# Three FFN heads put in order by hand: side 3's sums ahead of the tail, weight loads by free room, GpSimd's accumulating loads ahead of its power

## The chip, the cores and the metric

The kernel runs on one core of a Trainium2 chip. The metric is the device time of one execution in microseconds (us), the median of several executions. A core has five engines with a queue of instructions each, which go in order within an engine and wait for each other by semaphores: TensorE (PE; its weight loads are shown as PEld), VectorE (DVE), ScalarE (ACT), GpSimd (POOL) and SyncE (SP). Here SyncE issues the plain DMA loads, and GpSimd issues those that add to what lies in the buffer already (accumulating loads).

## The reference

A trunk of four layers on a sequence of 512 tokens with 1024 channels. Each layer is a mixer (S5 state space, gated linear attention (GLA), differential attention, S5 again) and an FFN, all float32:

```python
for layer in range(4):
    h = rmsnorm(x, norm_mix[layer]);  x = x + mixer(h)
    h = rmsnorm(x, norm_ffn[layer])
    g, u = split(h @ w_gate_up, 2)          # 1024 x (2 x 2816)
    x = x + (silu(g) * u) @ w_down          # 2816 x 1024
return rmsnorm(x, norm_final)
```

## The kernel before

Every float32 matrix is split into a rounded half and the residue (`halves`: a ScalarE cast and a VectorE subtraction, into a `whl` buffer, five of them), and a product is three TensorE matmuls: high by high, high by low, low by high.

The gate and up products of the FFN of layers 1, 2 and 3 are done by a scheme with seven products where plain blocking has eight. The activations, transposed, lie in four quarters `F[(0,0)]`, `F[(0,1)]`, `F[(1,0)]`, `F[(1,1)]` of a tile that the trace calls `halves`; `a11`, `a12`, `s` and `a22` are names for them. Seven combinations of the quarters, the sides "11", "12", "1", "2", "3", "4", "22", are split once per layer (`parts`, called by `side`). `total(name)` makes the sums by VectorE in place: "1" is `s - a22`, "2" then `s - a11`, "4" then `s + a12`. Before, "3" is made after "1" and "2", as `-s - a22`, in two buffers `s3`.

The weights go by 11 blocks of 256 hidden channels. A block has five weight tiles of 512 KB, loaded by `load(name, q, half, plus, room)`: "11", "21" and "22" are plain quarters; "1" and "3" are a plain load by SyncE (the base) and then an accumulating load by GpSimd that adds another quarter. "11" and "3" go into `wst` (three buffers), the others into buffers from the list `slots`, or into a given `room`. `added` adds "22" to "1" and `four` adds "21", on GpSimd for blocks 0 and 1 and on VectorE for the rest. `one`, `two`, `five`, `six`, `seven`, `three`, `four` are the seven products; `one_out`, `five_out`, `six_out` copy their sums out of PSUM. `one`, `six`, `seven` and `four` of a block use the PSUM bank `a`, `five` and `three` bank `c`, `two` bank `d`; in the trace all are on line 505.

The head of an FFN is the stretch from the last evacuations of the mixer's output projection (its tail; `add_x` calls `take` for each 128x512 piece of `x`) to the middle of block 2. In it the order is written out by hand (`self.hand(...)` opens the guard, an empty `self.hand()` ends it), for TensorE, ScalarE, VectorE and SyncE. GpSimd's order there, and all orders after it, are a scheduler's. The layer's row scale (`finish`: the mean square, then a power on GpSimd, line 124), its diagonal (`diag`) and its spread over the rows (`spread`, `rows`) lie between the products of blocks 0 and 1. `left.ahead(n)` loads and splits "11" of blocks 0 and 1 while the projection runs; the class is `Sides`, a `Left` with `early = True`.

At the start of `ffn` block 0's and block 1's tiles are loaded: block 0's "21" and "1" into slots, its "22" into the first half of a tile `lent`; block 1's "21" into the last slot, "1" into the second half of `lent`, "22" into the tile of the norm's gain, which is free after the last `take`. When the head is over, `halves` and the gain tile join the slots (`freed`), and block 2's "1" goes into `F[(0,1)]`, which `total("4")` is the last to read. In layer 2, `turn_x` stores `x` to DRAM and loads it back in another order by GpSimd's queue (`xturn`, 2 MB each way).

Of the kernel before, what the change touches and what calls it, by code (L numbers as in the profile page):

```python
# [11 lines left out]
F32 = mybir.dt.float32  # L12
# [4 lines left out]
ALU = mybir.AluOpType  # L17
# [4 lines left out]
P = 128  # L22
D = 1024
SEQ = 512
NT = SEQ // P
# [35 lines left out]
class Left:  # L61
# [15 lines left out]
    def room(self):  # L77
        self.hT = [self.tr.hp.tile([P, KT, SEQ], F32R, tag="hT", name=f"hT{z}") for z in range(2)]
# [14 lines left out]

    def square(self, t, d):
        tr = self.tr
        junk = tr.np_.tile([P, 512], F32, tag="h", name="sq")
        tr.nc.scalar.activation(
            junk[:], tr.x[:, t, d * 512 : (d + 1) * 512], AF.Square, scale=1.0 / 32.0,
            accum_out=self.ms[:, d, t : t + 1],
        )  # L100
# [25 lines left out]
    def diag(self):  # L126
        tr = self.tr
        nc = tr.nc
        self.dg = diag = tr.np_.tile([P, NT, P], F32, tag="h", name="diag")
        for t in range(NT):  # L130
            nc.vector.tensor_scalar(diag[:, t], tr.ident[:], self.r[:, t : t + 1], None, op0=ALU.mult)

# [11 lines left out]
class Sides(Left):  # L144
# [18 lines left out]
    def ahead(self, n):  # L163

        E = mybir.EngineType
        if not self.heads:
            self.tr.hand(E.PE, E.Activation, E.DVE, E.SP)
        w = [self.tr.staged(self.quarter(0, 0, b), 4, 256) for b in range(len(self.heads), len(self.heads) + n)]
        self.heads += [self.tr.halves(y, 4, 256) for y in w]

    def open(self, pool, names):

        for n in names:
            self.place[n] = pool.tile([P, 2, 4, 256], F32R, name="side" + n)
# [15 lines left out]
    def total(self, name):  # L190

        v = self.tr.nc.vector
        a11, a12, s, a22 = (self.F[k] for k in ((0, 0), (0, 1), (1, 0), (1, 1)))
        if name == "3":
            self.us = []
            for k in (0, 2):
                u = self.tr.np_.tile([P, 2, 256], F32, tag="h", name="s3")
                v.scalar_tensor_tensor(u[:], s[:, k : k + 2], -1.0, a22[:, k : k + 2], op0=ALU.mult, op1=ALU.subtract)
                self.us.append(u)
        else:  # L200
            y, op = {"1": (a22, ALU.subtract), "2": (a11, ALU.subtract), "4": (a12, ALU.add)}[name]
            v.tensor_tensor(s, s, y, op=op)
# [10 lines left out]
class Trunk:  # L213
# [81 lines left out]
    def gemm_b(self, stat, w, nk, c0, evac, k0=0, tail=0, between=(), ahead=None):  # L295
# [22 lines left out]
        if tail:  # L318
            hls = [self.wb(w, k0 + kb, c0) for kb in range(nk - tail, nk, 2)]
            if ahead:  # L320
                ahead()
            for t in range(NT):
                for j in range(tail):
                    k = nk - tail + j
                    self.mm3(
                        accs[t][:], stat(k, 0, t), stat(k, 1, t), hls[j // 2][:, 0, j % 2],
                        hls[j // 2][:, 1, j % 2], k == 0, k == nk - 1,
                    )
                evac(t, accs[t])
# [180 lines left out]
    def seven_block(self, fp, slots, left, wgu, b, turn):  # L510
# [3 lines left out]
        v = nc.vector  # L514
        A = left.place
        T = lambda name: fp.tile([P, 512], F32, tag="r1" if name == "r1" else "glu", name=name, bufs=2 if name == "r1" else 3)
        W, H, bank, keep, lent = {}, {}, {}, {}, set()
# [6 lines left out]
        def load(name, q, half, plus=None, room=None):  # L524
            if name in ("11", "3"):
                W[name] = self.staged(left.quarter(q, half, b), 4, 256)
            else:
                W[name] = slots.pop(0) if room is None else room
                if room is not None:
                    lent.add(name)  # L530
                nc.sync.dma_start(W[name][:], left.quarter(q, half, b))
            w = W[name]
            if plus:
                self.added = nc.gpsimd.dma_start(w[:], left.quarter(*plus, b), accum_op=ALU.add)
# [11 lines left out]
        def direct():  # L546
            load("11", 0, 0)

        def roomed(sums=None, rest=None):

            load("21", 1, 0)
            load("1", 0, 1, (0, 0), sums)
            load("22", 1, 1, None, rest)

        def summed():
            load("3", 0, 1, (1, 1))
# [50 lines left out]
        def four():  # L607
# [18 lines left out]
            return act  # L626

        return dict(
            split=split, direct=direct, roomed=roomed, summed=summed, one=one, one_out=one_out, two=two,
            two_out=two_out, gate1=gate1, five=five, five_out=five_out, added=added, six=six, six_out=six_out,  # L630
            seven=seven, three=three, four=four,
        )

    def ffn(self, l, left, after=None, turn=False, aside=None):

        i = self.i
        wgu, wd = i["ffn_w_gate_up"][l], i["ffn_w_down"][l]
        nxt = None
        r = left.r
        with self.tc.tile_pool(name=f"ffn{l}", bufs=1, reuse_waits="tile") as fp:  # L640

            room = lambda: fp.tile([P, 2, 4, 256], F32, tag="act", name="lent", bufs=4)
            left.open(fp, ("1", "2", "4", "3", "22") if l < 3 else ("1", "2"))
            if l == 3:
                lent = room()
            slots = [fp.tile([P, 4, 256], F32, name=f"slot{n}") for n in range(SLOTS)]

            if l < 3:
                lent = room()
            self.jobs = aside(fp) if aside else iter(())  # L650
            blocks = [self.seven_block(fp, slots, left, wgu, b, turn) for b in range(FFN_HIDDEN // 256)]
            f = blocks[:2]
            if l == 3:
                left.open(fp, ("4", "3", "22"))
            f[0]["roomed"](None, lent[:, 0])
            f[0]["summed"]()
            f[1]["roomed"](lent[:, 1], left.g[:].rearrange("p (k n) -> p k n", n=256))
            f[1]["summed"]()
            f[0]["split"]("21")
            f[0]["one"]()  # L660
            left.finish()
            f[1]["split"]("21")
            self.flush()
            f[1]["one"]()
            f[0]["one_out"]()
            left.total("1")
            left.diag()
            left.side("1")
            left.total("2")
            f[1]["one_out"]()  # L670
            f[0]["split"]("1")
            left.side("2")
            f[0]["two"]()
            left.spread()
            left.rows()
            f[1]["split"]("1")
            f[1]["two"]()
            f[0]["two_out"]()
            f[0]["five"]()
            f[0]["added"]()  # L680
            f[0]["split"]("1")
            f[1]["two_out"]()
            f[1]["five"]()
            f[1]["added"]()
            f[1]["split"]("1")
            f[0]["five_out"]()
            left.total("3")
            left.side("3")
            f[1]["five_out"]()
            f[0]["six"]()  # L690
            left.total("4")
            left.side("4")
            f[0]["six_out"]()
            f[1]["six"]()
            left.side("22")
            self.hand()
            slots += left.freed() + [left.g[:].rearrange("p (k n) -> p k n", n=256)]
            b0 = 0
            for nb in (4, 4, 3):
                acts = []  # L700
                for n in range(b0, b0 + nb):
                    b = blocks[n]
                    if n > 1:
                        b["direct"]()
                        b["roomed"]()
                        b["summed"]()
                    if turn and n == 2:

                        with self.tc.issue_after(self.added.ins):
                            r = self.turn_x(left.r)  # L710
                    todo = ["one", "one_out", "five", "five_out", "added", "six", "six_out", "two", "two_out"]
                    if n < 2:
                        todo = ["six_out"] if n else []
                    todo += ["gate1", "seven", "three"] if n > 1 else ["seven", "gate1", "three"]
                    for step in todo:
                        b[step]()
                    acts.append(b["four"]())
                    next(self.jobs, None)
                stat = lambda k, part, t: acts[k // 2][:, part, k % 2, t * P : (t + 1) * P]
                if nb == 3 and after is not None:  # L720
                    nxt = Left(self, after)
                for d in range(2):
                    tail = 4 if d == 1 and b0 == 8 else 0
                    self.gemm_b(stat, wd, 2 * nb, d * 512, self.add_x(d, nxt, r), k0=2 * b0, tail=tail)
                b0 += nb
            for _ in self.jobs:
                pass
        return nxt
# [1315 lines left out]
```

## Time and profile before

| | |
|---|---|
| Time, median of 3 (lowest to highest) | 2433.03 us (2430.8 to 2436.79) |
| The profiled execution: its own time | 2430.78 us |
| Its span in the profile | 2428.7 us |
| TensorE busy | 2281.9 us, 94% |
| VectorE, ScalarE, GpSimd busy | 61%, 44%, 14% |
| Mean granted TensorE clock | 0.974 |
| The three heads begin (first `one`) at | 875.5, 1519.5, 2060.2 us |

Times in the profile are us from the span's start. A row of a timeline has the start, the duration, the engine, the line, the operation, the tile written and those read, the shape and the count; in brackets stands the engine's idle time just before it and what ended it. A row of waits has the total, the count and the longest. "busy" means that an instruction was under way.

### The profile page before, as it was taken

The numbers are of one execution on the slowest core, as the hardware profiler recorded it, in microseconds if no ns is written. First come the engines' busy times: TensorE is split into PE (matmuls) and PEld (weight loads), VectorE is DVE, ScalarE is ACT, GpSimd is POOL, SyncE is SP. The second block draws the span as 40 slices with busy tenths as digits, with TensorE's granted clock in tenths as the row PEclk, the third lists the DMA queues.
The fourth block names the chain that finished last, engine by engine and source line by source line (L and its number), as shares of the span: only waits on it lengthen the run. The fifth ranks groups of instructions, "written<-read, shape, count | busy, mean of one in ns | idle before, by whom it ended". The sixth has DMA issues, their size and how long they took to land. (4 is left out here: it accounts for less than half of the span.)

```text
span 2428.7 us, 35189 instructions
## 1 busy us (share of the span) xinstructions
PE 2281.9 (94%) x14054; PEld 1975.6 (81%) x14054; DVE 1490.2 (61%) x2276; ACT 1071.3 (44%) x1740; POOL 328.9 (14%) x366
## 2 busy tenths in 40 slices
PE   4799999999999989999999998799999799899997
PEld 3578888788877779898987876799999688799996
DVE  7764655555424467585744675675755864767674
ACT  4453444444352355252535675453533223544442
POOL 4330101200100021010002130300000210301000
PEclk9699999999999999999999999899999899899999
DMA  4124343543422348574336463875632643865621
GB/s 110 33 62 134 100 142 135 165 154 135 140 79 79 109 114 201 133 181 114 105 118 151 101 139 104 203 205 130 183 87 79 231 142 109 187 182 140 173 71 69
DMA packets 275502, 317.42 MB, mean 131 GB/s; under 512 B 45653, under 2 KB 214377, under 8 KB 274058
## 3 DMA queue, kind: packets, MB, share of 16 engines
q1 hardware_dynamic: 227210, 238.14, 31.4%
q0 software_dynamic: 48128, 77.02, 15.5%
q8 instruction: 111, 1.82, 0.3%
q14 instruction: 53, 0.43, 0.1%
HBM read 275.92 MB, written 23.99 MB: 123 GB/s over the span
## 5 line engine op out<-in xcount | busy, mean ns | idle before, releaser
L277 DVE TENSOR_TENSOR whl<-wst,whl 128x1024 fp32r<-128x1024 f32 x294 | 359.9, 1226 | 359.3 <-ACT whl L276 358.3
L276 ACT CAST whl<-wst 128x1024 fp32r<-128x1024 f32 x294 | 308.3, 1050 | 526.2 <-PE acc L293 351.5
L505 PE MATMUL a<-side,whl 128*128 128x256 f32 x2376 | 298.9, 284 | 26.5 <-ACT r L595 26.5
L505 PEld LDWEIGHTS a<-side,whl 128*128 128x128 f32 x2376 | 289.9, 195 | 27.4 <-ACT r L595 27.3
L293 PE MATMUL acc<-whl,act 128*128 128x512 f32 x704 | 277.3, 394 | 0.0
L292 PE MATMUL acc<-whl,act 128*128 128x512 f32 x704 | 276.0, 392 | 0.0
L291 PE MATMUL acc<-whl,act 128*128 128x512 f32 x704 | 275.5, 391 | 0.0
L505 PE MATMUL c<-side,whl 128*128 128x256 f32 x1584 | 198.5, 282 | 15.8 <-ACT whl L276 13.6
L505 PEld LDWEIGHTS c<-side,whl 128*128 128x128 f32 x1584 | 191.5, 193 | 17.4 <-ACT whl L276 14.6
L292 PEld LDWEIGHTS acc<-whl,act 128*128 128x128 f32 x704 | 132.2, 188 | 29.4
L291 PEld LDWEIGHTS acc<-whl,act 128*128 128x128 f32 x704 | 132.2, 188 | 29.4 <-issue 0.7
L293 PEld LDWEIGHTS acc<-whl,act 128*128 128x128 f32 x704 | 132.3, 188 | 26.9
L291 PE MATMUL any<-hT,whl 128*128 128x512 f32 x384 | 151.7, 395 | 0.0
L293 PE MATMUL any<-hT,whl 128*128 128x512 f32 x384 | 149.6, 390 | 0.0
L292 PE MATMUL any<-hT,whl 128*128 128x512 f32 x384 | 149.6, 390 | 0.0
L291 PE MATMUL acc<-whl,hT 128*128 128x512 f32 x352 | 143.0, 406 | 1.0 <-ACT whl L276 0.6
L292 PE MATMUL acc<-whl,hT 128*128 128x512 f32 x352 | 138.1, 392 | 1.0 <-DVE whl L277 1.0
L293 PE MATMUL acc<-whl,hT 128*128 128x512 f32 x352 | 138.3, 393 | 0.0
L277 DVE TENSOR_TENSOR whl<-halves,whl 128x1024 fp32r<-128x1024 f32 x60 | 73.3, 1223 | 63.2 <-ACT whl L276 63.2
L277 DVE TENSOR_TENSOR whl<-slot,whl 128x1024 fp32r<-128x1024 f32 x63 | 82.4, 1309 | 46.8 <-ACT whl L276 46.8
L292 PE MATMUL acc<-whl,zT 128*128 128x512 f32 x256 | 104.1, 407 | 5.5 <-DVE whl L277 5.5
L291 PE MATMUL acc<-whl,zT 128*128 128x512 f32 x256 | 103.2, 406 | 2.7 <-ACT zT L407 2.7
(426 smaller groups left out, 4266.6 us busy)
## 6 DMA issues: line engine op xcount, KB each, us to landing
wst<-in_ffn_w_gate_up_dram SPq DMA_DIRECT2D x110, 512.0 KB, 3.8
wst<-in_ffn_w_down_dram SPq DMA_DIRECT2D x88, 512.0 KB, 4.0
halves<-in_ffn_w_gate_up_dram SPq DMA_DIRECT2D x42, 512.0 KB, 4.8
slot<-in_ffn_w_gate_up_dram SPq DMA_DIRECT2D x39, 512.0 KB, 4.4
wst<-in_ffn_w_gate_up_dram POOLq DMA_DIRECT2D x33, 512.0 KB, 6.4
wst<-in_s_w_glu_dram SPq DMA_DIRECT2D x32, 512.0 KB, 3.7
spill<-opsp POOLq DMA_DIRECT2D x8, 2048.0 KB, 8.8
wst<-in_gla_w_in_dram SPq DMA_DIRECT2D x24, 512.0 KB, 3.7
```

Source lines behind the costliest of these rows:

```text
L276: nc.scalar.copy(hl[:, 0], w[:])
L277: nc.vector.tensor_tensor(hl[:, 1], w[:], hl[:, 0].bitcast(F32), op=ALU.subtract)
L291: mm(out, lh, rh, start=first, stop=False)
L292: mm(out, lh, rl, start=False, stop=False)
L293: mm(out, ll, rh, start=False, stop=last)
L505: mm(o, hl[:, x, k, c], side[:, y, k], start=first and not (j or k or n), stop=k == 3 and n == 2, skip_group_check=True,)
```

## The change

- `total("3")` is called in `ahead`, as soon as both "11" are there, in the tail; it is `a11 - s` with the quarters as they came, a plain two-input subtraction, the same value as before up to rounding.
- Since its two buffers (tag "h") are now held through the tail, the squares of the second half of `x` are written into the buffer of `R`, and `diag` into an "hh" buffer.
- Order of the loads at the start of `ffn`: "21" and "1" of block 0, "21" and "1" of block 1, block 0's "22" and "3", block 1's "3", and last block 1's "22" into the gain tile. Both "1" now go into `lent`, and block 0's "22" into the third slot.
- GpSimd too keeps the written order within the guard: its four accumulating loads stand before the power of `finish`.

As built, the instructions outside the three heads keep their places on every engine but for a few neighbours. In the heads, `total("4")` stands ahead of the cast of block 0's "3" on VectorE; GpSimd's accumulating load for block 2's "1" (into `halves`) stands before the one for its "3" (into `wst`), and in layer 2 also before `xturn`, behind which it stood; TensorE's `five` of block 2 comes after `seven` and `four` of block 1.

```diff
     def square(self, t, d):
         tr = self.tr
-        junk = tr.np_.tile([P, 512], F32, tag="h", name="sq")
+        late = d and self.early
+        junk = tr.np_.tile([P, 512], F32, tag="R" if late else "h", name="sq", bufs=1 if late else 2)
...
-        self.dg = diag = tr.np_.tile([P, NT, P], F32, tag="h", name="diag")
+        self.dg = diag = tr.np_.tile([P, NT, P], F32, tag="hh" if self.early else "h", name="diag", bufs=2)
...
         if not self.heads:
-            self.tr.hand(E.PE, E.Activation, E.DVE, E.SP)
+            self.tr.hand(E.PE, E.Activation, E.DVE, E.SP, E.Pool)
...
         self.heads += [self.tr.halves(y, 4, 256) for y in w]
+        if len(self.heads) == 2:
+            self.total("3")
...
-                v.scalar_tensor_tensor(u[:], s[:, k : k + 2], -1.0, a22[:, k : k + 2], op0=ALU.mult, op1=ALU.subtract)
+                v.tensor_tensor(u[:], a11[:, k : k + 2], s[:, k : k + 2], op=ALU.subtract)
...
-        def roomed(sums=None, rest=None):
+        def roomed(sums=None):
             load("21", 1, 0)
             load("1", 0, 1, (0, 0), sums)
-            load("22", 1, 1, None, rest)
+        def rest(room=None):
+            load("22", 1, 1, None, room)
...
-            f[0]["roomed"](None, lent[:, 0])
+            f[0]["roomed"](lent[:, 0])
+            f[1]["roomed"](lent[:, 1])
+            f[0]["rest"]()
             f[0]["summed"]()
-            f[1]["roomed"](lent[:, 1], left.g[:].rearrange("p (k n) -> p k n", n=256))
             f[1]["summed"]()
+            f[1]["rest"](left.g[:].rearrange("p (k n) -> p k n", n=256))
...
             f[0]["five_out"]()
-            left.total("3")
             left.side("3")
...
                         b["direct"]()
                         b["roomed"]()
+                        b["rest"]()
                         b["summed"]()
```

More of the change, by code (lines that the diff above doesn't have):

```diff
@@ L628, in seven_block @@
         return dict(
-            split=split, direct=direct, roomed=roomed, summed=summed, one=one, one_out=one_out, two=two,
+            split=split, direct=direct, roomed=roomed, rest=rest, summed=summed, one=one, one_out=one_out, two=two,
             two_out=two_out, gate1=gate1, five=five, five_out=five_out, added=added, six=six, six_out=six_out,
```

## The prediction

> **What bounds the kernel now.** I read the page, then TensorE's waits, then the timeline of each engine around the three FFN heads.
>
> ```profile
> span 2428.7 us, 35189 instructions
> PE 2281.9 (94%) x14054; PEld 1975.6 (81%) x14054; DVE 1490.2 (61%) x2276; ACT 1071.3 (44%) x1740; POOL 328.9 (14%) x366
> ...
> PE a L505 <- ACT r L595: 26.5, 4, 9.7
> ...
> PE c L505 <- ACT whl L276: 13.6, 5, 4.1
> ...
> PE c L505 <- DVE whl L277: 2.3, 3, 0.8
> ```
>
> TensorE is busy for 94% of the span, so only its idle time can be won. The three rows of waits (L505 is the seven-product FFN) are 26.5 + 13.6 + 2.3 = 42.4 us of it. The timelines put all of them into the three heads. The head of layer 1 (H1), TensorE:
>
> ```profile
> 875.46 3.12 PE L505 MATMUL a<-sides,whl 128*128 128x256 f32 x24
> ...
> 892.45 0.50 PE L505 MATMUL c<-side,whl 128*128 128x256 f32 x2 [1.18 <-ACT whl L276]
> ...
> 909.27 5.49 PE L505 MATMUL a<-side,whl 128*128 128x256 f32 x24 [5.59 <-ACT r L595]
> ...
> 929.77 4.03 PE L505 MATMUL a<-side,whl 128*128 128x256 f32 x24
> ...
> 939.91 2.88 PE L505 MATMUL a<-side,whl 128*128 128x256 f32 x24
> ```
>
> 875.46 is `one` of block 0; then come idle stretches ahead of `five` of block 1, `seven` of block 0 (909.27) and block 2's first use of its "1"; 929.77 is `seven` of block 1, and from `six` of block 2 (939.91) TensorE runs without a gap. That last start is my yardstick: a head gains what it moves. ScalarE, SyncE, GpSimd, VectorE in H1:
>
> ```profile
> 891.36 1.04 ACT L276 CAST whl<-lent 128x1024 fp32r<-128x1024 f32 x1 [4.49 <-DMA lent<-in_ffn_w_gate_up_dram]
> ...
> 926.19 1.04 ACT L276 CAST whl<-halves 128x1024 fp32r<-128x1024 f32 x1 [5.37 <-DMA halves<-in_ffn_w_gate_up_dram]
> 876.81 0.37 SPq L531 DMA_DIRECT2D gain<-in_ffn_w_gate_up_dram  x1
> ...
> 907.68 4.86 SPq L531 DMA_DIRECT2D halves<-in_ffn_w_gate_up_dram  x3
> 879.52 1.93 POOL L124 TENSOR_TENSOR rcol<-ms,mhalf 128x4 f32<-128x4 f32 x1 [30.03 <-DVE ms L123]
> ...
> 882.23 1.81 POOL L534 DMA_DIRECT2D lent<-in_ffn_w_gate_up_dram  x1
> ...
> 886.52 3.38 POOL L588 TENSOR_TENSOR slot<-slot,lent 128x1024 f32<-128x1024 f32 x1 [1.19 <-DVE whl L277]
> 893.74 2.38 POOL L588 TENSOR_TENSOR lent<-lent,gain 128x1024 f32<-128x1024 f32 x1 [3.84 <-DVE whl L277]
> ...
> 907.55 1.29 POOL L534 DMA_DIRECT2D slot<-in_ffn_w_gate_up_dram  x1 [3.92 <-DMA slot<-in_ffn_w_gate_up_dram]
> 910.97 1.28 POOL L534 DMA_DIRECT2D wst<-in_ffn_w_gate_up_dram  x1 [2.13 <-DVE side L183]
> 913.34 1.30 POOL L534 DMA_DIRECT2D halves<-in_ffn_w_gate_up_dram  x1 [1.09 <-DMA halves<-in_ffn_w_gate_up_dram]
> 894.17 3.03 DVE L277 TENSOR_TENSOR whl<-slot,whl 128x1024 fp32r<-128x1024 f32 x1
> ...
> 900.69 3.48 DVE L198 SCALAR_TENSOR_TENSOR s<-halves 128x512 f32<-128x512 f32 x2
> 904.10 1.21 DVE L277 TENSOR_TENSOR whl<-wst,whl 128x1024 fp32r<-128x1024 f32 x1
> ...
> 906.44 1.21 DVE L202 TENSOR_TENSOR halves<-halves 128x1024 f32<-128x1024 f32 x1
> ```
>
> Two chains are to be seen. First, block 1's sum load ("1" in `lent`) is issued only at 882.23, behind GpSimd's power, and ScalarE waits for it until 891.36. Second, `total("4")` (VectorE, 906.44 to 907.65) frees a quarter of `halves`; SyncE then loads block 2's "1" into it (907.68), GpSimd adds the other quarter by an accumulating load (913.34), and ScalarE waits for that until 926.19, 12.85 us after its issue. ScalarE goes in order: the copy that `seven` of block 1 needs stands behind that cast, and TensorE resumes 3.6 us after the landing.
>
> **The change, step by step** (H1, on the clock above).
>
> *Loads and queues.* The bases of both "1", both "21", block 0's "22" and both "3" now go out ahead of the `gain` load, which still waits for the last use of the gain (876.81). GpSimd issues its four accumulating loads as the bases land, before the power instead of three of them behind it. They move some 20 us forward into the tail of the projection, where this window has the DMA idle, and cost nothing there:
>
> ```profile
> 860.00:870.00 10.00, 10.00 (x47) 8.25 (x46) 2.44 (x4) 1.38 (x4) 0.00 (x0) 1.00 0.00 0
> 852.89 1.22 DVE L277 TENSOR_TENSOR whl<-wst,whl 128x1024 fp32r<-128x1024 f32 x1
> ```
>
> (The last two numbers of the first row are DMA share and GB/s.) The power is now queued behind the loads, and `diag`, VectorE's next step, behind the power; the last base needs the buffer of block 0's "11", whose cast ends with the row at 852.89, so it lands far ahead of 879.52. Price taken: zero; if that cover went, every microsecond would go into the whole head. The wait of 4.49 at 891.36 goes, and next late is the port: GpSimd's add, 886.52 + 3.38 = 889.90.
>
> *VectorE's chain.* While GpSimd adds (2.38 us), VectorE's 128x1024 subtraction stands still: 3.03 us from 894.17, ending 1.08 after GpSimd's 896.12, where an undisturbed one takes 1.21. So from 889.90: cast residue of block 1's "1" to 890.98; GpSimd's second add 891.06 to 893.44; next residue 894.5; third add to 896.98; next residue 898.1. Then, without the two `s3` sums (3.48) that now lie in the tail: first half of side 3 0.6 (half of a 1.21 operation), to 898.7; GpSimd's fourth add takes the port to 901.1; second half 901.7; `total("4")`, which now stands ahead of the cast at 904.10, to 902.9. Before: 907.65. That is 4.8 us earlier. The two sums in the tail cost 1.2 us of VectorE, which waits for TensorE there; at worst they push one evacuation by that, taken as nothing. To keep their buffers free, the late squares write into `R` and `diag` into an `hh` buffer; one engine writes the squares in order and the transposes have read `hh` by then, so this costs nothing either.
>
> *The load that ends the head.* Base at 902.9 instead of 907.68. Landing of the base 5.66 later, as before: 908.6. GpSimd's order is now slot, `halves`, `wst` instead of slot, `wst`, `halves`: one 512 KB load less ahead of it. Bounds for issue to landing: 12.85 (above) and 8.2, from the slot row:
>
> ```profile
> wst<-in_ffn_w_gate_up_dram POOLq DMA_DIRECT2D x33, 512.0 KB, 6.4
> ...
> slot<-in_ffn_w_gate_up_dram POOLq DMA_DIRECT2D x12, 512.0 KB, 8.2
> ```
>
> I take the middle, 10.5, because one of two predecessors is gone while the DMA stays crowded: landing at 919.1, against 926.15.
>
> [...]
>
> *From landing to `six` of block 2.* ScalarE's cast 1.05, VectorE's residue 1.2, now ahead of the product that the next ScalarE copy needs (0.7), two ScalarE copies 0.6 each: `seven` of block 1 at landing + 4.2 (before + 3.6), 923.3. Fewer products of block 2 are done by then (11 of `one`, where 16 and two of `five` were), so 85 remain instead of 24 + 8 + 24 + 22 = 78. The chain of waits gives their pitch:
>
> ```profile
> 1602.00 2.72 PE c L505 x24
> ```
>
> 2.72 / 24 = 0.113 each: 9.6 us. The restart after idling cost 10.14 - 78 x 0.113 = 1.3 before; taken again (bounds: zero, and 3.2 as in H2 below). `six` at 923.3 + 9.6 + 1.3 = 934.2 against 939.91: **-5.7 in H1**. All other idle stretches (I get 3.6 instead of 5.59 ahead of `seven` of block 0) are hidden ahead of this landing.
>
> *The other heads.* H2 (layer 2) and H3 (layer 3):
>
> ```profile
> 1519.52 3.12 PE L505 MATMUL a<-sides,whl 128*128 128x256 f32 x24
> ...
> 1581.39 5.49 PE L505 MATMUL a<-side,whl 128*128 128x256 f32 x24 [9.72 <-ACT r L595]
> ...
> 1593.40 2.99 PE L505 MATMUL a<-side,whl 128*128 128x256 f32 x24
> 1557.57 1.30 POOL L734 DMA_DIRECT2D xturn<-vall  x1
> 1558.67 1.53 POOL L534 DMA_DIRECT2D halves<-in_ffn_w_gate_up_dram  x1
> 1578.87 1.04 ACT L276 CAST whl<-halves 128x1024 fp32r<-128x1024 f32 x1 [10.98 <-DMA halves<-in_ffn_w_gate_up_dram]
> 2060.16 3.11 PE L505 MATMUL a<-sides,whl 128*128 128x256 f32 x24
> ...
> 2124.90 2.88 PE L505 MATMUL a<-side,whl 128*128 128x256 f32 x24
> 2111.24 1.04 ACT L276 CAST whl<-halves 128x1024 fp32r<-128x1024 f32 x1 [5.58 <-DMA halves<-in_ffn_w_gate_up_dram]
> ```
>
> H3 is H1 shifted by 2060.16 - 875.46 = 1184.70: `six` at 2118.9 against 2124.90, **-6.0**. In H2 the accumulating load also stood behind the 2 MB `xturn` store (1557.57) and took 20.2 us; the build puts it ahead of `xturn` now. Shifted by 644.06: 1578.3 against 1593.40, **-15.1**. Restart price before, in H2: 12.01 - 78 x 0.113 = 3.2. The loads that are now behind `xturn` (block 3's) are wanted only 16 us after that start (six products of 2.72).
>
> **Sum:** -5.7 - 15.1 - 6.0 = -26.8. The profiled execution took 2430.78 (2.1 outside the span; 0.1% under the median 2433.03): 2430.78 - 26.8 = **2404**. With 12.85 and with 8.2 for the last landing the sum is -20 and -34: 2411 and 2397.
>
> **Rivals.** (A) *More*: in the quieter queue the accumulating load takes the 6.4 of its most common row and TensorE restarts at full rate. Per head 4.1 + 1.3 more: -26.8 - 16 = -43, 2388. For: base and sum fall earlier than the rest of the crowd; against: the same bytes still follow within 20 us. (B) *Given back in H2*: block 3's "1" and "3" sums now share GpSimd's queue with `xturn` and its reload, and come late. If one of them costs as much as `halves` did ahead of it (20.2 - 10.5 = 9.7) plus one restart (3.2), the gain is -14: 2417. For: the crowded queue; against: 16 us of products as cover. (C) *Not what it says*: the earlier order is void because a `lent` room is still occupied. Then the sum load lands as before, and only `s3` (3.48) and the place of the cast (1.2) go, partly under GpSimd's lock: about -3 per head, 2422. Against: both `lent` loads in H1 are issued back to back with slots that are free. (D) *Slower*: the DMA is limited by bytes, not by order, and the `halves` sum lands exactly when it did (926.2, 1578.8, 2111.2). Then `six` is 4.2 + 9.6 + 3.2 = 17.0 after it, the longer idling bringing the longer restart, against 13.8, 14.6 and 13.7 before: +3.2 + 2.4 + 3.3 = +9, 2440. It decides if the landing moves by less than 3 us per head; against it: `xturn` leaves the way in H2.
>
> **Numbers.** Forecast 0.60, A 0.12, B and C together 0.13, no measurable change 0.06 (a landing that moves by 2 to 5 us), D 0.09. What can be told from no change is about 0.3%, 7 us. Faster 0.85, same 0.06, slower 0.09. Range 2390 to 2422: it holds the forecast's 2397 to 2411, the near part of A, and B and C.
>
> **What would show it.** In the profile after: the ScalarE wait for `lent` (4.49) gone; the accumulating loads ahead of the power; no L198 operation in the head; `total("4")` some 5 us earlier against `one`; the `halves` sum landing about 44 us after the start of `one` in all heads (now 50.7, 59.3 and 51); TensorE's idle time ahead of `seven` of block 1 as the largest that is left. Wrong, if the power starts late, if the `halves` sum takes 13 us or more, or if TensorE waits in block 3 of layer 2.

## The result: 15 us faster, a little over half of what was forecast

| | before | after |
|---|---|---|
| Median (lowest to highest) | 2435.29 us (2430.8 to 2438.74), 5 runs | 2420.19 us (2413.49 to 2425.78), 5 runs |
| The profiled execution, its span | 2430.78, 2428.7 us | 2425.78, 2424.1 us |

The ratio is 0.9939, with a 95% interval of 0.9916 to 0.9961: the change gains 15.1 us where 26.8 were forecast. The profiled execution of after is the slowest of its five, so what follows compares stretches within the two profiles, not their ends. The page of after, and then TensorE's waits (total, count, longest):

```profile
span 2424.1 us, 35200 instructions
PE 2282.2 (94%) x14054; PEld 1975.2 (81%) x14054; DVE 1495.5 (62%) x2276; ACT 1070.4 (44%) x1740; POOL 329.8 (14%) x366
```

```profile
PE a L508 <- ACT r L600: 26.9, 6, 6.1
...
PE a L508 <- DVE r L604: 4.0, 2, 3.2
```

The waits for `whl` of 13.6 and 2.3 us in the heads (ScalarE's cast and VectorE's residue, ahead of bank c) are gone but for 0.2 us, and VectorE's residue now costs 2.9 us ahead of bank a, in six short waits, where it cost 0.8. At the same time the wait for the copy `r` (now line 600) stands where it stood, 26.9 against 26.5, in six places instead of four. A new one has come, for VectorE's `r` on line 604. TensorE's timeline shows the places; `one` of block 0, `seven` of block 0 (H1 only), `seven` of block 1 and `six` of block 2, and in H2 `four` of block 2 and the product behind it at the end:

```profile
880.48 3.12 PE L508 MATMUL a<-sides,whl 128*128 128x256 f32 x24
...
909.31 3.01 PE L508 MATMUL a<-side,whl 128*128 128x256 f32 x24 [3.26 <-ACT r L600]
...
929.18 5.49 PE L508 MATMUL a<-side,whl 128*128 128x256 f32 x24 [6.11 <-ACT r L600]
...
941.78 2.99 PE L508 MATMUL a<-side,whl 128*128 128x256 f32 x24
...
1526.00 3.11 PE L508 MATMUL a<-sides,whl 128*128 128x256 f32 x24
...
1574.80 5.43 PE L508 MATMUL a<-side,whl 128*128 128x256 f32 x24 [5.86 <-ACT r L600]
...
1587.08 2.88 PE L508 MATMUL a<-side,whl 128*128 128x256 f32 x24
...
1601.49 5.49 PE L508 MATMUL a<-side,whl 128*128 128x256 f32 x24 [3.21 <-DVE r L604]
1606.78 3.28 PE L508 MATMUL a<-sides,whl 128*128 128x256 f32 x24
...
2059.62 3.12 PE L508 MATMUL a<-sides,whl 128*128 128x256 f32 x24
...
2108.24 4.99 PE L508 MATMUL a<-side,whl 128*128 128x256 f32 x24 [5.02 <-ACT r L600]
...
2120.16 2.99 PE L508 MATMUL a<-side,whl 128*128 128x256 f32 x24
```

From `one` to `six`: 61.30 in H1 (before 64.45), 61.08 in H2 (73.88), 60.54 in H3 (64.74), 20.2 us less in all. But ahead of 1601.49, 11 us after H2's `six`, TensorE stands idle for 3.21 us, and the 24 products behind that take 5.29 until the next one starts (1606.78), instead of the 2.72 of the chain's row. So the stretch from `six` of H2 to `one` of H3 grows from 466.76 to 472.54: 5.8 are given back. -20.2 + 5.8 = -14.4, and the medians say -15.1. The two yardsticks account for the whole time within 2 us here and in seven of the ten kernels below; kernels 5, 8 and 9 are off by 3.1, 3.7 and 5.6. (In the profile after, H1 begins 5.0 us later than in the one before, and the way from H1's `six` to H2's `one` is 4.6 us longer. That code is untouched but for the two sums in the tail, and kernels 1, 6 and 9, which have them there too, begin H1 at 875.9 to 876.6; over the twelve profiles of this study H1 begins between 875.46 and 881.68.)

The head of H1 on the other engines, where the load lands that ends it (SyncE, VectorE, GpSimd, ScalarE):

```profile
907.72 0.37 SPq L534 DMA_DIRECT2D halves<-in_ffn_w_gate_up_dram  x1
906.48 1.21 DVE L205 TENSOR_TENSOR halves<-halves 128x1024 f32<-128x1024 f32 x1
884.53 1.94 POOL L125 TENSOR_TENSOR rcol<-ms,mhalf 128x4 f32<-128x4 f32 x1 [15.72 <-DVE ms L124]
...
909.82 1.31 POOL L537 DMA_DIRECT2D slot<-in_ffn_w_gate_up_dram  x1 [3.81 <-DMA slot<-in_ffn_w_gate_up_dram]
913.06 1.28 POOL L537 DMA_DIRECT2D halves<-in_ffn_w_gate_up_dram  x1 [1.94 <-DMA halves<-in_ffn_w_gate_up_dram]
914.49 1.29 POOL L537 DMA_DIRECT2D wst<-in_ffn_w_gate_up_dram  x1
925.08 1.05 ACT L279 CAST whl<-halves 128x1024 fp32r<-128x1024 f32 x1 [7.16 <-DMA halves<-in_ffn_w_gate_up_dram]
...
928.55 0.58 ACT L600 COPY r<-a 128x512 f32<-128x512 f32 x1
```

`total("4")` (906.48) ends 27.2 us after `one`, the base is issued there and has landed when GpSimd adds to it (913.06), and that accumulating load lands at 925.07, 12.0 us after its issue and 44.6 after `one`. The copy that `seven` of block 1 needs (928.55) stands behind its cast. And this is the way to H2's new wait, by the same engines:

```profile
1560.99 1.67 POOL L741 DMA_DIRECT2D xturn<-vall  x1
...
1588.71 1.30 POOL L537 DMA_DIRECT2D gain<-in_ffn_w_gate_up_dram  x1 [25.29 <-DMA gain<-in_ffn_w_gate_up_dram]
1562.96 3.09 SPq L534 DMA_DIRECT2D gain<-in_ffn_w_gate_up_dram  x1
1597.27 1.05 ACT L279 CAST whl<-gain 128x1024 fp32r<-128x1024 f32 x1 [5.63 <-DMA gain<-in_ffn_w_gate_up_dram]
1598.35 1.23 DVE L280 TENSOR_TENSOR whl<-gain,whl 128x1024 fp32r<-128x1024 f32 x1 [4.08 <-ACT whl L279]
...
1600.76 0.68 DVE L604 TENSOR_TENSOR r<-r,a 128x512 f32<-128x512 f32 x1
```

The base of block 3's "1" goes into the gain tile at 1562.96, two microseconds behind the 2 MB of `xturn`, and lands some 25 us later; GpSimd waits 25.29 for it, adds (1588.71), and ScalarE's cast waits until 1597.27. VectorE takes the residue and only then the subtraction on line 604, which has nothing to do with block 3's "1" but stands behind it in VectorE's order, and which frees bank a for `four` of block 2.

### The profile page after: what moved, and what is told of

Its sections match the earlier page's. It is cut to its first block, busy times and chain, and to the rows that moved or that the text cites. A ratio compares the mean times of both kernels' runs of the same rounds, so it can differ in the third digit from the quotient of the medians.

```text
span 2424.1 us, 35200 instructions
## 1 busy us (share of the span) xinstructions
PE 2282.2 (94%) x14054; PEld 1975.2 (81%) x14054; DVE 1495.5 (62%) x2276; ACT 1070.4 (44%) x1740; POOL 329.8 (14%) x366
## 3 DMA queue, kind: packets, MB, share of 16 engines
q0 software_dynamic: 48128, 77.02, 15.4%
## 5 line engine op out<-in xcount | busy, mean ns | idle before, releaser
L508 PE MATMUL a<-side,whl 128*128 128x256 f32 x2376 | 301.5, 285 | 33.9 <-ACT r L600 26.9
L508 PE MATMUL c<-side,whl 128*128 128x256 f32 x1584 | 191.9, 277 | 0.2 <-DVE whl L280 0.2
L508 PEld LDWEIGHTS c<-side,whl 128*128 128x128 f32 x1584 | 186.3, 188 | 0.4 <-DVE whl L280 0.4
L296 PEld LDWEIGHTS acc<-whl,act 128*128 128x128 f32 x704 | 132.3, 188 | 26.9
L295 PE MATMUL acc<-whl,zT 128*128 128x512 f32 x256 | 103.9, 406 | 5.2 <-DVE whl L280 5.2
L294 PE MATMUL acc<-whl,zT 128*128 128x512 f32 x256 | 103.1, 405 | 2.7 <-ACT zT L410 2.7
L296 PE MATMUL acc<-whl,zT 128*128 128x512 f32 x256 | 103.6, 406 | 1.2 <-DVE zT L411 1.2
```

The source lines that it names most:

```text
L294: mm(out, lh, rh, start=first, stop=False)
L295: mm(out, lh, rl, start=False, stop=False)
L296: mm(out, ll, rh, start=False, stop=last)
L508: mm(o, hl[:, x, k, c], side[:, y, k], start=first and not (j or k or n), stop=k == 3 and n == 2, skip_group_check=True,)
```

## The experiments

My theory after this reading: the heads end with the landing of block 2's accumulating load, and what was missed is the give-back in layer 2 plus two terms that were sized too small (the accumulating load, the restart). The rivals: that the gain has another maker than the change's order of loads, that the landing does not matter because another operand is as late, that order in the DMA queues does not matter because the bytes are the limit.

All runs by the two yardsticks of TensorE, against the profile before (heads 203.07 us in sum, `six` of H2 to `one` of H3 466.76). "Measured" is the median less the median of the kernel before in the same comparison; the ratio on record is not exactly the quotient of these two medians (kernel 4's 0.998 would be -4.9 us, kernel 3's 0.9946 would be -13.1).

| kernel | three heads | six H2 to one H3 | sum | measured | ratio (95% interval) |
|---|---|---|---|---|---|
| the change | -20.2 | +5.8 | -14.4 | -15.1 | 0.9939 (0.9916 to 0.9961) |
| 1 xturn later | -21.3 | +3.8 | -17.5 | -16.9 | 0.9931 (0.9913 to 0.9948) |
| 2 other buffer | -38.8 | +13.4 | -25.4 | -25.8 | 0.9888 (0.9871 to 0.9904) |
| 3 sums alone | -13.6 | +0.8 | -12.8 | -11.8 | 0.9946 (0.9928 to 0.9963) |
| 4 loads alone | -3.5 | -0.8 | -4.3 | -3.3 | 0.998 (0.9968 to 0.9993) |
| 5 = 2 and xturn later | -39.1 | +10.1 | -29.0 | -25.9 | 0.9893 (0.9875 to 0.9912) |
| 6 = 2 and xturn early | -39.8 | -0.2 | -40.0 | -39.8 | 0.9839 (0.982 to 0.9858) |
| 7 copy ahead of the cast | -23.6 | +8.2 | -15.4 | -17.2 | 0.9922 (0.9901 to 0.9942) |
| 8 = 2 and block 0 first | -35.3 | +15.8 | -19.5 | -15.8 | 0.9932 (0.9913 to 0.9951) |
| 9 own queue | -26.0 | +5.5 | -20.5 | -26.1 | 0.9894 (0.9879 to 0.9909) |
| 10 xturn early alone | -21.0 | -0.3 | -21.3 | -20.4 | 0.9914 (0.9896 to 0.9932) |

**The two parts of the change (3 and 4).** Kernel 3 is the kernel before with the sums moved, in the form and the buffers that they have in the change; kernel 4 is the change with the sums put back, in their form and buffers of before:

```diff
 # 3, from the kernel before
         self.heads += [self.tr.halves(y, 4, 256) for y in w]
+        if len(self.heads) == 2:
+            self.total("3")
...
-            left.total("3")
             left.side("3")
```

> The kernel before, with side 3's sums alone moved ahead of the tail as plain differences (buffers for the squares and diag as in the change); the loads keep their order and GpSimd its schedule. Theory (the 3.48 us of the two sums lie whole on VectorE's chain): total("4") about 28.7 us after `one` instead of 32.2, the landing and `six` of block 2 3 us earlier in the heads of layers 1 and 3 and up to 3 in layer 2, where the accumulating load stays behind xturn; 2435 - 9 = 2426 us. [...]

> The changed kernel with side 3's sums back in the head, in their form and buffers of before; only the order of the loads and GpSimd's place in the written order are left of the change. Theory: total("4") about 30.7 us after `one` (1.5 less than before, the sums being 3.5 of the 5.0); the accumulating load in layer 2 no longer behind xturn; heads of layers 1 and 3 -1.5 us each, layer 2 -7 net, because the wait for block 3's "1" there stands at a time that xturn sets and so takes less when the head ends later; 2435 - 10 = 2425 us. Rival (the parts add up): 2435 - 6 = 2429 us, since the sums alone would be 9 of the 15. Second rival (all of the gain is the loads'): 2420 us.

The sums alone give 11.8, the loads alone 3.3. That these make the 15.1 of both to the tenth is chance: the intervals of the two ratios are 8.5 and 6 us wide, and the yardsticks give -12.8 and -4.3. For kernel 3 the theory came near in size (-9 expected, -11.8 measured), but not by its mechanism: H1 and H3 gain 1.7 and 2.3, where 3 each was expected, and H2 gains 9.6, where up to 3 was. For kernel 4 the rival that adds up the parts came nearest (-6 expected). What I had not seen is in H2. GpSimd and ScalarE in H2, kernel 3 and then kernel 4:

```profile
1563.96 1.28 POOL L537 DMA_DIRECT2D halves<-in_ffn_w_gate_up_dram  x1 [2.00 <-issue]
...
1566.29 1.20 POOL L736 DMA_DIRECT2D xturn<-vall  x1
...
1574.70 1.05 ACT L279 CAST whl<-halves 128x1024 fp32r<-128x1024 f32 x1 [5.03 <-DMA halves<-in_ffn_w_gate_up_dram]
```

```profile
1558.62 1.30 POOL L739 DMA_DIRECT2D xturn<-vall  x1
1560.28 1.29 POOL L534 DMA_DIRECT2D halves<-in_ffn_w_gate_up_dram  x1 [0.36 <-DMA halves<-in_ffn_w_gate_up_dram]
...
1579.85 1.04 ACT L276 CAST whl<-halves 128x1024 fp32r<-128x1024 f32 x1 [12.25 <-DMA halves<-in_ffn_w_gate_up_dram]
```

With the sums moved, the accumulating load stands ahead of `xturn` and takes 10.7 us (1563.96 to 1574.7); without, it stands behind, although GpSimd has its place in the written order, and takes 19.6 (1560.28 to 1579.85). It is issued behind the guard, so it is the scheduler that places it; probably by when it reckons the base to be there, which the two sums made earlier, but no run shows the scheduler's reason. So the large gain in H2 (73.88 to 64.31 in kernel 3) is the sums' doing. The wait of 4.49 for `lent`, which the loads' order takes away, was worth little by itself: in kernel 4 H1 and H3 take 64.86 and 64.57, as before. In its H1 `total("4")` ends 2.7 us earlier than before and the sum lands 2.2 earlier (48.5 after `one`), but `six` of block 2 follows 16.3 behind the landing instead of 13.7, so the head gains nothing. In H1 of kernel 3 it follows 16.5 behind, and of 4.4 us at the landing 1.7 are left at `six`.

**When the 2 MB cross (1 and 10).** `turn_x` one block later; then, apart from that, its store at the head's start and its reload behind block 3's sums:

```diff
 # 1
-                    if turn and n == 2:
+                    if turn and n == 3:
 # 10: the same, and the two stores taken out of turn_x into turn_out
-            f[0]["one_out"]()
+            f[0]["one_out"](), turn and self.turn_out(left.r)
```

> The changed kernel, with the 2 MB store xturn and its reload issued behind block 3's sums instead of behind block 2's. Theory (the gain of the head of layer 2 is given back because block 3's "1" stands behind xturn): the base of that "1", 25.3 us in flight in the changed kernel, lands within some 10 us, TensorE's wait of 3.21 us ahead of `four` of block 2 and its slow restart go, the stretch from `six` of block 2 in layer 2 to `one` of layer 3 falls from 472.5 to about 467 us; 2420 - 6 = 2414 us. Rival (bytes, not order): the 2 MB cross the same crowd later and the wait comes back in block 3 or 4; 2420 us. Second rival: the reloaded x comes too late for the first sum into x at the end of block 3; 2425 us or more.

Kernel 1 loses the wait of 3.21 and gains 2.0 on the stretch, not 5.8; its 2414.65 meets the theory's 2414, but in a comparison in which the kernel before, too, was 3.8 us faster (2431.53). The rest is paid at a new place, much as the first rival had it: the weights of the down-projection, issued at 1602.39, land at 1611.2. ScalarE waits for them and holds up block 3's gate, and TensorE waits behind it:

```profile
1611.24 1.05 ACT L279 CAST whl<-wst 128x1024 fp32r<-128x1024 f32 x1 [5.07 <-DMA wst<-in_ffn_w_down_dram]
...
1615.23 0.80 PE L294 MATMUL acc<-whl,act 128*128 128x512 f32 x1 [2.64 <-DVE g L546]
```

> The changed kernel, with xturn's store at the start of the head of layer 2 and its reload behind block 3's sums (as in the sixth experiment, without the swap of buffers). Theory (the forecast's failed step is the give-back in layer 2): the wait of 3.21 us with its 2.6 us of restart goes and nothing takes its place; the three heads keep their 60.5 to 61.3 us from `one` to `six`, and the time is what the heads alone are worth: 2420 - 6 = 2414 us, ratio to before 0.991. Rival (the give-back is of other making, or is paid elsewhere again as in the first experiment): 2417 to 2420 us.

Kernel 10 has neither wait: 466.48 from `six` of H2 to `one` of H3, where before has 466.76, and the heads as in the change. Its 20.4 are what the heads are worth (2416.59 against 2436.94 for the kernel before in that comparison, ratio 0.9914 where 0.991 was expected). In the changed kernel the give-back was the crossing of `xturn` with block 3's "1": without it the whole 5.8 is gone.

**The buffer that block 2's "1" waits for (2), and the same with xturn moved (5 and 6).**

```diff
 # 2
-                    b = blocks[n]
+                    b, slots[:] = blocks[n], [slots[k] for k in (0, 6, 2, 3, 4, 5, 1, 7)] if n == 2 else slots
```

> The changed kernel, with two buffers swapped: block 2's "1" goes into slot 0 (free when GpSimd's third add of the head has ended, some 21.6 us after `one`) and block 4's "21" into the quarter of `halves` that total("4") frees 27.2 us after `one`. Theory (the head ends with the landing of block 2's accumulating load, which is set by when its buffer comes free and by what is ahead in GpSimd's queue): the base is issued 5 to 6 us earlier and its accumulating load is the first of its queue; it lands 36 to 39 us after `one` instead of 44.3 to 44.6, TensorE's idle stretch of 5 to 6 us ahead of `seven` of block 1 shrinks to under 2, the restart price of 2.3 to 3.0 to about 1, and `six` of block 2 starts 53 to 56 us after `one` instead of 60.5 to 61.3; three heads, 2420 - 3 x 6 = 2402 us. Rival (the DMA is limited by bytes): the landing moves by less than 3 us, 2413 to 2420 us. Second rival: another operand of `seven` comes as late as the landing does now; 2418 us.

The heads take 54.23, 55.07 and 55.00, the middle of the theory's range: the landing does set them. But the earlier H2 is through, the longer it waits at the same place, since `xturn` sets that time. GpSimd and ScalarE in H1 of kernel 2, and TensorE in H2:

```profile
906.26 1.31 POOL L537 DMA_DIRECT2D slot<-in_ffn_w_gate_up_dram  x1
...
919.24 1.05 ACT L279 CAST whl<-slot 128x1024 fp32r<-128x1024 f32 x1 [1.08 <-issue]
...
1592.13 5.45 PE L508 MATMUL a<-side,whl 128*128 128x256 f32 x24 [11.09 <-DVE r L604]
```

The accumulating load goes out at 906.26, 25.5 us after `one` (880.75), as the first of its queue, and the cast of the sum starts 38.5 us after `one` instead of 44.6. The idle time of 11.09 us and the slow start behind it give back 13.4 of the 38.8 that the heads gained.

> The second experiment's kernel (block 2's "1" in slot 0) with xturn and its reload issued behind block 3's sums, as in the first. Theory: TensorE's wait of 11.09 us ahead of `four` of block 2 in layer 2 (block 3's "1" behind xturn), with 2.7 us of slow restart, goes; the down-projection after block 3 is then kept waiting by its weights, which follow the 2 MB, as in the first experiment (2.64 us and some 1.6 of restart) or by up to twice that, since it begins earlier; 2406 - 14 + 6 = 2398 us. Rival (bytes): all of the 14 us come back ahead of the down-projection; 2406 us.

Here the rival of bytes was right in the time (2407.45 where it had 2406), and nearly in the place: 10.1 of the 13.4 come back ahead of the down-projection, in two waits of 2.62 and 4.52 us.

> The second experiment's kernel with xturn's store taken apart from its reload: the store goes out at the start of the head of layer 2, right behind GpSimd's power, where the windows of the changed kernel show the DMA at a share of 0.00 to 0.31 for 24 us; the reload stands behind block 3's sums. Theory (the give-back is a matter of when the 2 MB cross): neither block 3's "1" nor the down-projection's weights are late, the wait of 11.09 us and its restart of 2.7 go and nothing takes their place; 2406 - 14 = 2392 us. Rival: the store delays the gain's load and block 2's "21" in the head, or the reload alone still holds up the down-projection by 4 us; 2396 to 2400 us.

Kernel 6 is the fastest of all, 2393.52 us, as forecast to 1.5 us; as a gain over the kernel before it is 39.8, where the forecast meant 43. Its GpSimd queue and ScalarE, and then TensorE's waits:

```profile
1518.36 0.82 POOL L741 DMA_DIRECT2D xturn<-vall  x1
...
1562.65 1.29 POOL L537 DMA_DIRECT2D gain<-in_ffn_w_gate_up_dram  x1 [8.24 <-DMA gain<-in_ffn_w_gate_up_dram]
1572.32 1.05 ACT L279 CAST whl<-gain 128x1024 fp32r<-128x1024 f32 x1 [0.99 <-PE d L508]
```

```profile
PE a L508 <- ACT r L600: 13.3, 6, 3.3
```

The store goes out at 1518.36, at a point of the head where the DMA of the changed kernel stands at a share of 0.00 to 0.31; block 3's "1" is cast at 1572.32, waiting for TensorE by then and not for a DMA; the wait for the copy `r` has fallen from 26.9 to 13.3.

**Does TensorE need the landing, or does it only stand behind it (7)?**

```diff
 # 7; r2 of block 1 in a buffer of another pool
-            f[1]["six"]()
+            f[1]["six"](), f[1]["six_out"]()
...
-                        todo = ["six_out"] if n else []
+                        todo = []
```

> The changed kernel, with the copy that `seven` of block 1 needs put right behind block 0's in the written order, ahead of ScalarE's cast of block 2's "1" (its result goes to a buffer of another pool, so that nothing else moves). Theory (TensorE does not need the sum at that point, it only waits because ScalarE goes in order): the idle stretch of 5 to 6 us ahead of `seven` of block 1 and its restart go; block 1's `seven`, `three` and `four` run ahead of the landing, 44.5 us after `one`, so `six` of block 2 starts 52 to 55 us after `one` instead of 60.5 to 61.3; the wait in block 3 of layer 2 grows by as much as that head gains, so two heads count: 2420 - 2 x 7 = 2406 us. Rival (the landing is needed as soon in any case): TensorE idles as long ahead of `five` of block 2; 2418 to 2420 us.

`seven` of block 1 no longer waits, but the heads gain only 2.7, 0.5 and 0.2 more than the change's. TensorE and VectorE in H1:

```profile
926.88 4.58 PE L508 MATMUL a<-side,whl 128*128 128x256 f32 x24 [4.27 <-DVE r L604]
923.70 1.23 DVE L280 TENSOR_TENSOR whl<-halves,whl 128x1024 fp32r<-128x1024 f32 x1 [4.17 <-ACT whl L279]
...
926.05 0.68 DVE L604 TENSOR_TENSOR r<-r,a 128x512 f32<-128x512 f32 x1
```

One product further on, `four` of block 1 waits for line 604 (926.05), which stands in VectorE's order behind the residue of the very load (923.70). The theory is right that TensorE does not need the sum there, and the rival is right on the time: it is held by two engines that go in order, and freeing one moves the wait by one product.

**What the accumulating load waits for (9).** Behind the guard, block 4's accumulating load is put behind block 2's in GpSimd's queue:

```diff
+    if n == 4:
+        with tr.tc.issue_after(tr.hold.ins):   # hold: the accumulating load of block 2's "1"
+            b["roomed"]()
...
```

> The changed kernel, with two issues swapped in GpSimd's queue in each head: the accumulating load of block 2's "1" ahead of block 4's instead of behind it. The loads, their bytes and all SyncE issues stay. Theory (the 12.0, 10.9 and 11.7 us that it took are the crowd's: from 6 us after its issue on, the windows show the DMA at a share of 0.93 to 1.18): issue to landing falls by at most 2 us, `six` of block 2 by as much, 2420 - 4 = 2416 us. Rival (only the loads ahead in GpSimd's own queue count, 6 us each): it falls to about 7 us and each head gains 4 to 5 us, 2420 - 9 = 2411 us, the head of layer 2 losing its gain again to block 3's "1".

GpSimd and ScalarE in H1:

```profile
909.05 1.31 POOL L537 DMA_DIRECT2D halves<-in_ffn_w_gate_up_dram  x1 [6.96 <-DMA halves<-in_ffn_w_gate_up_dram]
...
919.49 1.04 ACT L279 CAST whl<-halves 128x1024 fp32r<-128x1024 f32 x1 [5.49 <-DMA halves<-in_ffn_w_gate_up_dram]
```

Issue to landing is 10.4 in H1 (12.0 in the change), 10.8 in H2 (11.0) and 9.9 in H3 (11.7); the landing comes 42.9, 43.0 and 42.9 us after `one`, 1.7, 1.3 and 1.6 earlier than in the change. The theory's "at most 2" holds, the rival's 5 does not. The windows of the change's profile fit the theory (last columns: granted clock, DMA share, GB/s):

```profile
908.00:914.00 6.00, 4.69 (x41) 4.69 (x42) 6.00 (x7) 5.58 (x7) 2.24 (x2) 1.00 0.93 279
914.00:920.00 6.00, 5.18 (x45) 5.02 (x44) 6.00 (x7) 1.58 (x2) 1.63 (x2) 1.00 1.15 232
920.00:926.00 6.00, 3.07 (x26) 2.85 (x25) 1.60 (x3) 0.92 (x1) 0.00 (x0) 1.00 1.18 238
926.00:932.00 6.00, 2.82 (x13) 2.82 (x14) 5.84 (x7) 3.33 (x6) 0.00 (x0) 0.67 0.84 261
```

The DMA's share is 0.93 to 1.18 in the three windows in which the load crosses (913.06 to 925.07). The rival's reading, by which only the loads ahead in GpSimd's own queue count, is not borne out by this run: as the first of that queue the load took 1.6, 0.2 and 1.8 us less than as the second. In H2 the give-back is as large as in the change (+5.5), but it stands elsewhere. TensorE, SyncE and ScalarE in H2 of kernel 9:

```profile
1584.19 3.01 PE L508 MATMUL a<-side,whl 128*128 128x256 f32 x24 [0.74 <-DVE r L604]
...
1595.78 4.58 PE L508 MATMUL a<-side,whl 128*128 128x256 f32 x24 [2.99 <-ACT r L572]
1550.27 0.37 SPq L534 DMA_DIRECT2D gain<-in_ffn_w_gate_up_dram  x1
1593.68 1.04 ACT L279 CAST whl<-wst 128x1024 fp32r<-128x1024 f32 x1 [4.22 <-DMA wst<-in_ffn_w_gate_up_dram]
```

The base of block 3's "1" (1550.27) is again issued 2.3 us behind `xturn`, but it takes 12.0 us instead of 25.7, and the wait ahead of `four` of block 2 falls from 3.21 to 0.74. Instead `six` of block 3 waits 2.99 us for a copy (line 572) that stands behind ScalarE's cast of block 3's "3", whose accumulating load went out behind `xturn`'s reload and took 14.2 us. So it is not `xturn` alone that settles which of block 3's loads comes late; what else does stays open. The time gained is more than the yardsticks show (-26.1 against -20.5). From profile to profile it is 21.0, so the other 5 us lie between profiles and medians (the kernel before took 2436.94 in that comparison and 2430.78 in its profile); more is not known.

**Block 0 first (8).** The residue of block 0's "3" ahead of `total("4")` (`seven` then takes the tile as already split), and its copy of bank a ahead of side 4, on top of kernel 2:

```diff
-            f[0]["six"]()
+            f[0]["six"](), f[0]["split"]("3")
             left.total("4")
+            f[0]["six_out"]()
             left.side("4")
-            f[0]["six_out"]()
```

> The second experiment's kernel with two things of block 0 ahead of side 4 in the written order: the residue of its "3" ahead of total("4"), and the copy of bank a ahead of ScalarE's cast of side 4. Theory (the idle 3.3 us ahead of `seven` of block 0 are ScalarE's wait for total("4"), which is late now only because block 2's "1" no longer hangs on it): that idle falls to about 1.5 and the restart behind it, 0 to 2.5 us by the traces, goes; layers 1 and 3 gain 2 to 4 us each, layer 2 nothing (its wait in block 3 stands at a time that xturn sets); 2406 - 6 = 2400 us. Rival: side 4, later by the two steps, stops `three` of block 0 for as long; 2406 us.

Theory and rival both missed (2400 and 2406 expected, 2417.47 measured). It came out slower than kernel 2, 0.9932 against 0.9888 of the kernel before. The idle time ahead of `seven` of block 0 fell only to 3.23, 2.36 and 2.36 us, a wait of 2.00 for line 604 came ahead of `four` of block 1 in H1 (57.73 instead of 54.23), and the wait in block 3 of H2 grew to 14.01. In H1 line 604 stands in VectorE's order behind `added` of block 2 (line 593), which had waited for a load into `halves`:

```profile
927.28 1.23 DVE L593 TENSOR_TENSOR slot<-slot,halves 128x1024 f32<-128x1024 f32 x1 [2.14 <-DMA halves<-in_ffn_w_gate_up_dram]
```

That this load is late because side 4, later by the two steps, frees its quarter later is likely, but no run shows it; `three` of block 0, where the rival saw the price, waits 0.50 in H2 and not at all in H1 and H3. The yardsticks account for 5.9 of the 10.0 us between kernels 2 and 8, of which 3.5 are H1's and 2.4 the wait in block 3; the rest is open.

## Why the prediction was wrong in size

**Right.** The mechanism in the heads, by its own steps. `total("4")` ends 27.2 us after `one` (forecast 27.4). The base lands 5.3 after its issue (5.66). GpSimd's power is not late (884.53, its four loads out ahead of it), the wait for `lent` is gone, no operation of the old line 198 is in the head. `seven` of block 0 waits 3.26 to 3.34 (3.6). `seven` of block 1 starts 4.1, 4.5 and 4.1 us after the landing (4.2). What the prediction calls a port and a lock is in the traces this: in the three heads of both profiles a 128x1024 subtraction of VectorE that starts while GpSimd adds takes 3.03 to 3.13 us instead of 1.21 to 1.23 and ends 1.1 us after the add; what holds it back, no run shows.

**Two terms of the sum were too small**, together 6.7 us by the yardsticks (-20.2 for the heads, forecast -26.8). The accumulating load: 12.0, 11.0 and 11.7 from issue to landing instead of 10.5, the landing 44.6, 44.3 and 44.5 after `one` instead of 43.6. The restart: `seven` of block 1 to `six` of block 2 is 12.60, 12.28 and 11.92, less 9.6 of products that is 3.0, 2.7 and 2.3 instead of 1.3. From the landing to `six` it is 16.7, 16.8 and 16.0: rival D had 17.0 for this stretch, the forecast 15.1. The 1.3 was read off a row that was not the same step: in H1 before, TensorE was held by block 2's "1" in bank c and had begun again 2.5 us ahead of the `seven` at which I began to count (927.28 instead of 929.77), so part of the price was paid outside. The bound of 3.2, from H2, was the like case, since there the idle time ended at `seven`. H1 came to -3.2, H2 to -12.8, H3 to -4.2 (forecast -5.7, -15.1, -6.0).

**One step failed**, and it is worth the other 5.8: "The loads that are now behind `xturn` (block 3's) are wanted only 16 us after that start", taken as free. The cover was counted to the product that uses the data. But the cast and the residue of that tile stand in the orders of ScalarE and VectorE ahead of block 2's evacuation (line 604), which TensorE wanted 11 us after the start; and the base was 25 us in flight. This is rival B, in its place, and half by its mechanism: B had the accumulating load late in GpSimd's queue, and here that took 8.5 us, while the plain base ahead of it came late. That B's -14 for the whole is near the measured -15.1 is luck: it priced the give-back at 12.9, where 5.8 was paid, and the heads fell short by 6.7 for other reasons. The 2420.19 lies inside the stated range only because B and C had widened it. Kernel 10 shows the step by itself: without the crossing the change is worth 20.4 us.

**Not told apart** in the prediction: which part of the change takes the accumulating load out from behind `xturn`. Kernels 3 and 4 show that the sums do, by moving the scheduler's order. Rival C had priced the sums without the loads at 2422, -9; they are worth 11.8, and the order of the loads, with the wait of 4.49 that the prediction put first, 3.3.

Rival A fell (no landing near 6.4 us), C fell as such (the early loads are early), D fell: the landing moved by 6.1, 15.0 and 6.5 us against `one`, far beyond its 3.

## What to carry to other kernels

A load that comes late stops not only the product that uses it but everything behind its cast on each engine that goes in order (here the subtraction on line 604, for which TensorE idled 3.21 us): count the cover to the first thing queued behind the cast. A price for starting again after idle time must be read from where the idle time ends, and at more than one place: the same 3.33 us cost 0.3 to 3.0. When an edit moves a queue's order, see what else crosses in that time: here a 2 MB store put into the nearly idle DMA of the head's start (a share of 0.00 to 0.31), together with a buffer that comes free 5 us earlier, brought another 25 us on top of the change's 15.

## What was not expected of the hardware

Whether starting again costs anything is not settled by the length of the idle time alone. Over the twelve profiles, TensorE was idle for 3.2 to 3.35 us in the heads 28 times; counted from the first start to the start of the 49th product, less idle time in between, eleven times the next 48 products ran at nearly full rate (0.42 us or less above 48 x 0.113), 17 times they took 1.7 to 3.0 us more. In the 32 places where it had been idle for 3.5 us or longer, the price was 1.6 or more. Shorter stretches were often free, but not always: behind 2.36 us in two heads of kernel 8 it was 1.1 and 1.7, behind 3.17 in kernel 9 it was 3.0. In the rows of after, 24 products took 3.01 us behind 3.26 of idle time and 5.49 behind 6.11, with a granted clock of 0.67 in the window from 926. Stretches of the same 3.33 us cost 0.3, 1.7 and 3.0 (H1 of kernel 10, H3 of after, H2 of kernel 2), and all 27 stretches between 3.5 and 6.8 us cost 1.6 or more. What decides it for a shorter stretch, no run shows.

The same accumulating load of 512 KB took 9.9 to 10.8 us as the first of its queue (kernel 9), 11.0 to 12.0 as the second (after), and 12.4 and 12.85 as the third (before, H3 and H1); behind the 2 MB store it took 19.6 (kernel 4) and 20.2 (before, H2). While it crossed in H1 and H3 of before and after, the windows have the DMA at a share of 0.93 to 1.18.
